# Layer 0's feed-forward up half: seven products on halved operands, its output through DRAM, and other buffer sizes

## The chip, the cores and the metric

The kernel runs on one core of a Trainium2 chip. The metric is device microseconds of one execution. Engines: TensorE (PE) for matmuls, VectorE (DVE), ScalarE (ACT), GpSimd (POOL), and SyncE (SP), whose queue issues most DMAs. Each engine works through its own queue in order and waits there on semaphores of the others.

## The reference

Two layers over 512 latent tokens (x) and 256 context tokens (ctx) of width 1024. Layer 0 mixes tokens by retention, layer 1 by differential attention; behind each mixer stands a gated feed-forward. Every sublayer is wrapped in RMS norms, with shift, scale and gate from SiLU(c) for the latents and SiLU(c_ctx) for the context:

```
u    = modulate(rms_norm(h, norm_g[l, 2]), shift, scale)
gate, val = split(u @ w_up)                  # 1024 -> 2 x 2816
h    = h + g * rms_norm((silu(dwconv3(gate) + b) * val) @ w_down, norm_g[l, 3])
```

dwconv3 is a convolution of three taps along the tokens, per channel. shift, scale and the gates of both layers are products of a 1024-vector with 6 x 1024 columns (adaLN). All is float32.

## The kernel before, in words

**Float32 on PE.** Every operand is split into a high half (a copy on ACT, rounded) and a low half (a subtraction on DVE, sometimes POOL): `split`, lines 58 to 60. A product is then three matmuls into the same PSUM bank: high x high, high x low, low x high (`mm3`, lines 96 to 99). A group with line 60 of the profile is thus a low half on DVE, one with line 59 a high half on ACT.

**Weights.** `W` (line 67) loads 128x1024 of raw weights by a DMA on SP into `wraw`, a pool of three buffers (line 63), and splits it into `wH`, `wL` (two buffers each) or, if `late`, into other tiles (`wlH`, `wlL`). With AHEAD a split stands earlier in the queues than the code has it.

**adaLN in the background.** 80 units are left over after the start; `ada_next(n)` (line 530) emits the next n. A unit loads 128x1024 of raw weights into the same `wraw` pool, and DVE multiplies and sums it against the conditioning vectors `cb` in one instruction (line 164) for each of one or two vectors: the output of the first goes to `adaj`, that of the last over `wraw` itself. The buffer is free after the last. In layer 0's retention (four heads, loop at 560 to 706) `ada_next(2)` stands behind the q and behind the k projection, `ada_next(3)` behind v, `ada_next(2)` behind the gates: 36 units. The other 44 lie in the up half, one pass of `between` behind each of its weights.

**Retention, per head.** q and then k: two column blocks c of 128 features, each eight contraction steps x three matmuls of 512 latent columns (into `psqx`) and of 256 context columns (`psqc`). Rotary operations on DVE (`ra`, `rb`, lines 591 to 593) need both column blocks. Then come gates, scores, values, and the normalised output, which goes to DRAM (`yTd`).

**Retention output and what follows** (`sublayer_out`, line 718). Latent tokens first, 16 contraction blocks; then, in a loop over the same 16 blocks, the context tokens, while a table `side` lets the other engines finish the latent tokens: gate and residual (`ft`, `hn`), norm (`xn`), PE transposes (`pst`) and modulation (`uf`) into the operand `UT`, whose halves lie in 24 tiles of 128x512 from the pool `s2`. The context tokens' norm and transposes come last (`ctx_part`), behind the first products of the next stage.

**Layer 0's up half** (`FFNUp`, line 282; called at 808 to 823). For each of 22 blocks f of 128 features, the gate unit and the value unit are each the sum over eight contraction blocks of matmuls with 512 and with 256 columns, into a bank each. Behind them: the convolution (ACT, and two operations on DVE, reading PSUM), SiLU on ACT, and the product with val on DVE, into tiles that stay in SBUF (`hTx`, `hTc`) for the down half (`sublayer_out` again, 22 contraction blocks).

A scheduler sets the order in each queue from the order in the code and the priorities; pools with few buffers add waits.

Of the kernel before, what the change touches and what calls it, by code (L numbers as in the profile page):

```python
# [30 lines left out]
def tile_hybrid_backbone(ctx: ExitStack, tc: tile.TileContext, A, out, dbg=None):  # L31
# [163 lines left out]
    class UT:  # L195
        def __init__(self):
            self.xH = [s2(F32R, name="uxH") for _ in range(KT)]
            self.xL = [s2(F32R, name="uxL") for _ in range(KT)]
            self.cH = self.cL = None

        def add_ctx(self):
            self.cH = [s2(F32R, (P, 2, 256), name="ucH") for _ in range(4)]
            self.cL = [s2(F32R, (P, 2, 256), name="ucL") for _ in range(4)]

        def part(self, p, k):

            if p == "c":
                return self.cH[k // 2][:, k % 2, :], self.cL[k // 2][:, k % 2, :]
            if isinstance(p, int) and p >= 4:
                o = slice((p - 4) * P, (p - 3) * P)  # L210
                return self.cH[k // 2][:, k % 2, o], self.cL[k // 2][:, k % 2, o]
            o = slice(p * P, (p + 1) * P) if isinstance(p, int) else {
                "x": slice(0, 512), "g0": slice(0, 256), "g1": slice(256, 512)}[p]
            return self.xH[k][:, o], self.xL[k][:, o]
# [8 lines left out]
    def to_u(ps, n, k, u, p, layer, sub_i, v):  # L223

        sh, sc = (0, 1) if sub_i == 0 else (3, 4)
        H, L = u.part(p, k)
        uf = t2((P, n), name="uf")
# [3 lines left out]
        else:  # L231
            nc.vector.tensor_scalar(out=uf, in0=ps, scalar1=a, scalar2=b, op0=ALU.mult, op1=ALU.add)
        split(H, L, uf)
# [127 lines left out]

    l0 = tc.tile_pool(name="l0", bufs=1)
# [32 lines left out]
    def ada_w(k):  # L395
        for kh in range(2):
            wada[k, kh] = W(A["ada0"][k * 2 + kh], late=k % 2 == 1, eng=nc.gpsimd if 2 * k + kh in (5, 9, 13, 4, 6, 0) else None, big=True)
# [69 lines left out]
    def first_ctx():  # L467
        U.add_ctx()
        norm_pair(psp, U, "c", xs[4:6], 0, 0)
# [8 lines left out]
    cb = l0p.tile([P, 2, 1024], F32, name="cb")  # L478
# [90 lines left out]
    for h in range(4):  # L569
# [3 lines left out]
        for qi in range(2):  # L573
# [29 lines left out]
            ada_next(2)  # L603
# [72 lines left out]
        ada_next(3)  # L676
# [25 lines left out]
        ada_next(2)  # L702
# [6 lines left out]
    def load_y(lo, hi):  # L709
        def at(k):  # L710
            y = s2(name="yin")
            nc.sync.dma_start(out=y[:, : hi - lo], in_=yTd[k, :, lo:hi])
# [5 lines left out]
    def sublayer_out(nk, unit, lx, lc, chunk, prev, dst_x, dst_c, layer, sub_i, hook, pre):  # L718
# [703 lines left out]
```

## Time and profile before

| | |
|---|---|
| median of three runs | 2206.97 us (2206.02 to 2208.29) |
| profiled execution | 2208.85 us, span 2207.0 us |
| PE busy | 2150.1 us, 97% |
| DVE, ACT, POOL busy | 56%, 38%, 11% |
| mean granted clock of PE | 0.986 |
| layer 0's up half | from 880.7 to about 1250 us |

The profile is one execution. A group row gives the mean length of one instruction; in a timeline, consecutive instructions of an engine overlap a little, so the distance of their starts is the cost of one. The word in brackets at the end of a timeline row is the idle time in front of it and what ended that. "issue to landing" of a DMA is from its issue on the queue until its data can be read.

### The profile page before, as it was taken

How to read it: one execution, taken by the hardware profiler on the slowest of the kernel's cores; microseconds unless marked ns; L12 is line 12 of the kernel's file. 1: busy time of each engine (PE TensorE's matmuls, PEld its weight loads, DVE VectorE, ACT ScalarE, POOL GpSimd, SP SyncE). 2: the span in 40 equal slices, each digit the busy share in tenths (PEclk: the TensorE clock that was granted, in tenths of full speed). 3: DMA queues.
4: the chain of work that ended last, by engine and by line, in shares of the span. 5: the costliest groups of instructions: out<-in, count | busy, mean ns of one | idle time of the engine just before them, and what ended most of it. 6: DMA issues, size and time to landing. Idle time of an engine off the chain costs nothing. (4 is left out here: it accounts for less than half of the span.)

```text
span 2207.0 us, 28221 instructions
## 1 busy us (share of the span) xinstructions
PE 2150.1 (97%) x11136; PEld 1834.2 (83%) x11136; DVE 1227.3 (56%) x1928; ACT 849.1 (38%) x1494; POOL 243.1 (11%) x310
## 2 busy tenths in 40 slices
PE   7999999999999999999999999999999789999998
PEld 6888888888888888888888888888888678888887
DVE  6656553553553348665445625767797686444524
ACT  5432233332332346322222324654455465333412
POOL 3001101100200101000000001021232151000000
PEclk8999999999999999999999999999999899999999
DMA  7232322322223366434444435611111332333333
GB/s 261 87 111 86 129 78 69 118 92 69 101 86 110 113 212 205 141 117 140 125 128 126 151 105 194 207 51 46 44 44 32 112 122 101 102 97 99 109 97 124
DMA packets 82732, 250.68 MB, mean 114 GB/s; under 512 B 10104, under 2 KB 13480, under 8 KB 82472
## 3 DMA queue, kind: packets, MB, share of 16 engines
q1 hardware_dynamic: 79880, 241.00, 34.0%
q0 software_dynamic: 2720, 7.89, 0.9%
q8 instruction: 87, 1.43, 0.3%
q14 instruction: 45, 0.37, 0.1%
HBM read 232.05 MB, written 16.80 MB: 113 GB/s over the span
## 5 line engine op out<-in xcount | busy, mean ns | idle before, releaser
L60 DVE TENSOR_TENSOR wL<-wraw,wH 128x1024 fp32r<-128x1024 f32 x233 | 286.1, 1228 | 504.9 <-ACT wH L59 503.3
L59 ACT ACTIVATE wH<-wraw 128x1024 fp32r<-128x1024 f32 x259 | 273.9, 1058 | 642.9 <-PE psa L99 182.9
L97 PE MATMUL psf<-uxH,wH 128*128 128x512 f32 (+1 forms) x672 | 258.7, 385 | 0.0
L98 PE MATMUL psf<-uxL,wH 128*128 128x512 f32 (+1 forms) x672 | 258.5, 385 | 0.0
L99 PE MATMUL psf<-uxH,wL 128*128 128x512 f32 (+1 forms) x672 | 258.1, 384 | 0.1
L97 PE MATMUL pso<-wH,lxH 128*128 128x512 f32 x432 | 168.3, 390 | 0.6 <-ACT grow L183 0.3
L98 PE MATMUL pso<-wL,lxH 128*128 128x512 f32 x432 | 168.1, 389 | 0.0
L99 PE MATMUL pso<-wH,lxL 128*128 128x512 f32 x432 | 168.1, 389 | 0.0
L164 DVE CUSTOM_DVE_ANT_0 wraw<-wraw,cb 128x1024 f32<-128x1024 f32 x80 | 97.6, 1223 | 96.9 <-DMA wraw<-in_ada_rest_dram 96.3
L99 PEld LDWEIGHTS psf<-uxH,wL 128*128 128x128 f32 x672 | 126.3, 188 | 25.6 <-DVE wL L60 0.3
L97 PEld LDWEIGHTS psf<-uxH,wH 128*128 128x128 f32 x672 | 126.5, 188 | 23.9
L98 PEld LDWEIGHTS psf<-uxL,wH 128*128 128x128 f32 x672 | 126.5, 188 | 23.4
L97 PE MATMUL psa<-wH,uxH 128*128 128x512 f32 x352 | 137.0, 389 | 0.0
L98 PE MATMUL psa<-wL,uxH 128*128 128x512 f32 x352 | 137.0, 389 | 0.0
L99 PE MATMUL psa<-wH,uxL 128*128 128x512 f32 x352 | 136.9, 389 | 0.0
L137 POOL TENSOR_SCALAR st<-st 128x1 f32<-128x1 f32 x42 | 27.7, 658 | 675.4 <-ACT junk L136 673.9
L97 PEld LDWEIGHTS pso<-wH,lxH 128*128 128x128 f32 x432 | 81.1, 188 | 17.8 <-ACT grow L183 0.6
L99 PEld LDWEIGHTS pso<-wH,lxL 128*128 128x128 f32 x432 | 81.1, 188 | 17.0
L99 PE MATMUL psf<-ucH,wL 128*128 128x256 f32 x336 | 95.1, 283 | 0.0
L98 PE MATMUL psf<-ucL,wH 128*128 128x256 f32 x336 | 95.1, 283 | 0.0
L98 PEld LDWEIGHTS pso<-wL,lxH 128*128 128x128 f32 x432 | 81.1, 188 | 16.6
L97 PE MATMUL psf<-ucH,wH 128*128 128x256 f32 x336 | 94.9, 282 | 0.0
(360 smaller groups left out, 5104.9 us busy)
## 6 DMA issues: line engine op xcount, KB each, us to landing
wraw<-in_up_dram SPq DMA_DIRECT2D x88, 512.0 KB, 3.6
wraw<-in_ada_rest_dram SPq DMA_DIRECT2D x80, 512.0 KB, 3.7
wraw<-in_down_dram SPq DMA_DIRECT2D x66, 512.0 KB, 3.6
wraw<-in_ret_in_dram SPq DMA_DIRECT2D x64, 512.0 KB, 3.7
wraw<-in_ret_out_dram SPq DMA_DIRECT2D x32, 512.0 KB, 3.8
wraw<-in_diff_in_dram SPq DMA_DIRECT2D x24, 512.0 KB, 3.6
wraw<-in_ada_dram SPq DMA_DIRECT2D x16, 512.0 KB, 7.3
wraw<-in_diff_out_dram SPq DMA_DIRECT2D x16, 512.0 KB, 3.8
```

Of the source, the lines that this page charges most:

```text
L59: nc.scalar.activation(out=h, in_=x, func=AF.Copy)
L60: (eng or nc.vector).tensor_tensor(out=l, in0=x, in1=h.bitcast(F32), op=ALU.subtract)
L97: nc.tensor.matmul(ps, l[0], r[0], start=first, stop=False)
L98: nc.tensor.matmul(ps, l[0], r[1], start=False, stop=False)
L99: nc.tensor.matmul(ps, l[1], r[0], start=False, stop=last)
L137: nc.gpsimd.tensor_scalar(out=s[:, 2:3], in0=s[:, 0:1], scalar1=s[:, 1:2], scalar2=EPS, op0=ALU.add, op1=ALU.add)
L164: nc.vector.tensor_tensor_reduce(out=o, in0=raw, in1=cb[:, v, :], scale=1.0, scalar=0.0, op0=ALU.mult, op1=ALU.add, accum_out=adaF[:, laye ...
```

## The change

The up half of layer 0 is rewritten as a scheme with seven products (`Seven`, `seven_w`, `ffn0`). The contraction is halved (features 0 to 511 and 512 to 1023), the columns are halved into the gate and the value block, and the tokens into two sets of 384 (two of every four latent blocks and one of two context blocks). In each pass f there are seven products of 4 contraction blocks x 3 matmuls x 384 columns, in the order 1, 6, 5, 7, 2, 3, 4.

- Token sums: per latent block of `sublayer_out`'s loop (`x_part`, at steps 6, 8, 10, 12) and for the context (`ctx_part`) one subtraction on POOL, three on DVE, and seven splits.
- Weight sums: four on POOL (S1 to S4, 128x512), seven splits of 128x512 per pass. The value block's raw weights go into an `s6` tile.
- Result sums: two copies of PSUM on ACT, five adds from PSUM on DVE, two adds on POOL, all of 384 columns. The gate lies in SBUF then, and the convolution reads it there.
- The result `val` goes to DRAM (`hd`) by a DMA on POOL's queue in each pass, and the down half loads it back on SP as it loads `yTd`.
- `ada_next` in retention goes from 2, 2, 3, 2 to 3, 3, 4, 3 per head (52 units); in the up half one unit stands behind each of the first 16 passes, and the last 12 behind them all.
- Pools: `s2` 48 to 31 buffers, `s6` 8 to 16; `UT` in eight `s6` tiles; the attention accumulators and some late weights in `s6`; `cb` in a pool of its own; the pool `l0` ends ahead of the up half.

The core of the diff:

```diff
-        return sp.tile(list(shape), dt, tag="s2", name=name, bufs=48)
+        return sp.tile(list(shape), dt, tag="s2", name=name, bufs=31)
 
     def s6(dt=F32, shape=(P, 1536), name="s6"):
-        return sp.tile(list(shape), dt, tag="s6", name=name, bufs=8)
+        return sp.tile(list(shape), dt, tag="s6", name=name, bufs=16)
...
-            ada_next(2)
+            ada_next(3)
...
-        ada_next(3)
+        ada_next(4)
...
-        ada_next(2)
+        ada_next(3)
...
-                4: lambda: (keep(2), sc(2)), 5: lambda: (keep(3), sc(3), tr(0)), 8: lambda: tr(1)}
+                4: lambda: (keep(2), sc(2)), 5: lambda: (keep(3), sc(3))}
+        if seven:
+            side |= {6 + 2 * q: lambda q=q: u.x_part(q, xn) for q in range(4)}
+        else:
+            side[5] = lambda: (keep(3), sc(3), tr(0))
+            side[8] = lambda: tr(1)
...
+        def sums(self, lo1, hi1, lo2, hi2, shape, at):
+
+            T = [t2(shape, name="T") for _ in range(2)]
+            a, b, c, d = (x[:, i] for x in T for i in range(2))
+            nc.gpsimd.tensor_tensor(out=b, in0=hi2, in1=hi1, op=ALU.subtract)
+            sub(a, hi1, lo1)
+            sub(c, hi2, a)
+            sub(d, lo2, c)
+            for i, x in ((1, lo1), (2, lo2), (3, hi2), (5, a), (6, c), (7, b), (4, d)):
+                split(at(self.H[i]), at(self.L[i]), x)
...
+    def seven_w(f):
+
+        g, v = load_raw(A["up"][0, 2 * f]), load_raw(A["up"][0, 2 * f + 1], True)
+        ops = {}
+        with tc.high_priority(offset=AHEAD):
+            g1, g2, v1, v2 = g[:, :512], g[:, 512:], v[:, :512], v[:, 512:]
+            S1, S2, S3, S4 = (t2(name="S") for _ in range(4))
+            pool = nc.gpsimd.tensor_tensor
+            pool(out=S1, in0=v1, in1=v2, op=ALU.add)
+            pool(out=S2, in0=S1, in1=g1, op=ALU.subtract)
+            pool(out=S3, in0=g1, in1=v1, op=ALU.subtract)
+            pool(out=S4, in0=g2, in1=S2, op=ALU.subtract)
+            for i, x in zip(ORDER, (g1, S2, S1, S3, g2, S4, v2)):
+                if i in (1, 2):
+                    H, L = (wp.tile([P, 1024], F32R, tag=t, name=t, bufs=2)[:, :512] for t in ("wH", "wL"))
+                else:
+                    H, L = s2(F32R, name="opH"), s2(F32R, name="opL")
+                split(H, L, x)
+                ops[i] = H, L
+        return ops
...
+            def product(i, p):
+                if i not in banks:
+                    banks[i] = bank("psf")
+                o = {"x": slice(0, 256), "c": slice(256, 384), "all": slice(0, 384)}[p]
+                H, L = ops[i]
+                for k in range(4):
+                    s = slice(k * P, k * P + P)
+                    mm3(banks[i][:, o], (H[:, s], L[:, s]), u.at(i, k, p), k == 0 and p != "c", k == 3 and p != "x")
...
+            if f == 0:
+                for i in ORDER[:4]:
+                    product(i, "x")
+                ctx_part()
+                for i in ORDER[:4]:
+                    product(i, "c")
+            for i in ORDER:
+                if f > 0 or i in ORDER[4:]:
+                    product(i, "all")
+                ps = banks[i][:, :384]
+                add = lambda o, a, b, e=nc.vector: e.tensor_tensor(out=o, in0=a, in1=b, op=ALU.add)
+                if i == 1:
+                    p1 = tmp("p1")
+                    nc.scalar.activation(out=p1, in_=ps, func=AF.Copy)
+                elif i == 6:
+                    u2 = tmp("u2")
+                    add(u2, ps, p1)
+                elif i == 5:
+                    p5, u4 = tmp("p5"), tmp("u4")
+                    nc.scalar.activation(out=p5, in_=ps, func=AF.Copy)
+                    add(u4, u2, p5, nc.gpsimd)
+                    if f + 1 < NF:
+                        nxt.append(seven_w(f + 1))
+                elif i == 7:
+                    u3, v = tmp("u3"), wide("val")
+                    add(u3, ps, u2)
+                    add(v[:, :, 1, :], three(u3), three(p5), nc.gpsimd)
+                elif i == 2:
+                    g = wide("gate3")
+                    add(g[:, :, 0, :], three(ps), three(p1))
+                elif i == 3:
+                    add(g[:, :, 1, :], three(ps), three(u4))
+                else:
+                    add(v[:, :, 0, :], three(ps), three(u3))
+            flat = lambda x: x.rearrange("p a b c -> p (a b c)")
+            g, v = flat(g), flat(v)
+            c = flat(wide("conv3"))
+            w0, w1, w2, cbias = (cw[:, 0, f, i : i + 1] for i in range(4))
+            nc.scalar.activation(out=c, in_=g, func=AF.Identity, scale=w1, bias=cbias)
+            for a, b in ((0, 512), (512, 768)):
+                nc.vector.scalar_tensor_tensor(out=c[:, a + 1 : b], in0=g[:, a : b - 1], scalar=w0, in1=c[:, a + 1 : b],
+                                               op0=ALU.mult, op1=ALU.add)
+                nc.vector.scalar_tensor_tensor(out=c[:, a : b - 1], in0=g[:, a + 1 : b], scalar=w2, in1=c[:, a : b - 1],
+                                               op0=ALU.mult, op1=ALU.add)
+            nc.scalar.activation(out=c, in_=c, func=AF.Silu)
+            nc.vector.tensor_tensor(out=v, in0=v, in1=c, op=ALU.mult)
+            nc.gpsimd.dma_start(out=hd[f], in_=v)
+            ada_next(1 if f < NF - 6 else 0)
+            ops = nxt[0] if nxt else None
...
+    ffn0(u, first, ctx_part)
     ada_next(len(ada_list))
...
-        NF, lambda k: A["down"][0, k], lhs_x(lambda k: F.hx[k]), lhs_c(lambda k: F.hc[k]), 5, lambda t: rows(h1d, t),
+        NF, lambda k: A["down"][0, k], lhs_x(load_y(hd, 0, 512)), lhs_c(load_y(hd, 512, 768)), 5, lambda t: rows(h1d, t),
```

**SP's queue in retention**, a head's v projection to the next head's k projection. `in_ret_in` is a retention weight, `in_ada_rest` an ada unit. Before:

```order
L64 DMA wraw<-in_ada_rest_dram 128x1024 x3
L64 DMA wraw<-in_ret_in_dram 128x1024 x4
L64 DMA wraw<-in_ada_rest_dram 128x1024 x2
L64 DMA wraw<-in_ret_in_dram 128x1024 x2
L64 DMA wraw<-in_ada_rest_dram 128x1024 x2
L64 DMA wraw<-in_ret_in_dram 128x1024 x3
L64 DMA wraw<-in_ada_rest_dram 128x1024 x2
```

After:

```order
L64 DMA wraw<-in_ada_rest_dram 128x1024 x4
L64 DMA wraw<-in_ret_in_dram 128x1024 x4
L64 DMA wraw<-in_ada_rest_dram 128x1024 x3
L64 DMA wraw<-in_ret_in_dram 128x1024 x2
L64 DMA wraw<-in_ada_rest_dram 128x1024 x3
L64 DMA wraw<-in_ret_in_dram 128x1024 x3
L64 DMA wraw<-in_ada_rest_dram 128x1024 x3
```

Each group of ada loads is longer by one, and the groups behind the q projection, the k projection and the gates are now as long as the pool is wide.

**DVE's queue behind the q projection of a head** (from the second `ra`, in front of which stands the first `rb`). Rows with `adaj` or `wraw` at line 164 are reductions of ada units. Before:

```order
L591 TENSOR_TENSOR ra<-psqx,rcos 128x512
L593 TENSOR_TENSOR ra<-ra,rb 128x512
L592 TENSOR_TENSOR rb<-psqx,rsin 128x512
L164 ISA adaj,adaF<-wraw,cb 128x1024
L164 ISA adaF 128x1
L164 ISA adaj,adaF<-wraw,cb 128x1024
L164 ISA adaF 128x1
L593 TENSOR_TENSOR ra<-ra,rb 128x512
L60 TENSOR_TENSOR qxL<-ra,qxH 128x512
L60 TENSOR_TENSOR wL<-wraw,wH 128x1024
L164 ISA wraw,adaF<-wraw,cb 128x1024
L164 ISA adaF 128x1
```

After:

```order
L593 TENSOR_TENSOR ra<-psqx,rcos 128x512
L595 TENSOR_TENSOR ra<-ra,rb 128x512
L594 TENSOR_TENSOR rb<-psqx,rsin 128x512
L164 ISA adaj,adaF<-wraw,cb 128x1024
L164 ISA adaF 128x1
L164 ISA adaj,adaF<-wraw,cb 128x1024
L164 ISA adaF 128x1
L595 TENSOR_TENSOR ra<-ra,rb 128x512
L60 TENSOR_TENSOR qxL<-ra,qxH 128x512
L164 ISA adaj,adaF<-wraw,cb 128x1024
L164 ISA adaF 128x1
L164 ISA wraw,adaF<-wraw,cb 128x1024
```

A third unit's first reduction stands ahead of the first unit's second one, and the weight's low half (`wL`) that stood in between is no longer there.

**DVE's queue in the up half**, one pass. Before (`hT` is the product with val):

```order
L328 TENSOR_TENSOR hTx<-psf,conv 128x512
L164 ISA wraw,adaF<-wraw,cb 128x1024
L164 ISA adaF 128x1
L328 TENSOR_TENSOR hTc<-psf,conv 128x256
L60 TENSOR_TENSOR wL<-wraw,wH 128x1024
L323 SCALAR_TENSOR_TENSOR conv<-psf,cw,conv 128x511
L325 SCALAR_TENSOR_TENSOR conv<-psf,cw,conv 128x511
L164 ISA adaj,adaF<-wraw,cb 128x1024
L164 ISA adaF 128x1
L164 ISA wraw,adaF<-wraw,cb 128x1024
L164 ISA adaF 128x1
L60 TENSOR_TENSOR wL<-wraw,wH 128x1024
```

After (`opL`, `wL` are low halves of operands, `u`, `gate`, `val` the result sums):

```order
L935 TENSOR_TENSOR u_9852<-psf,p_9837 128x384
L60 TENSOR_TENSOR opL<-S,opH 128x512 x4
L935 TENSOR_TENSOR gate_9941<-psf,p_9837 128x3x128
L60 TENSOR_TENSOR opL<-wraw,opH 128x512
L935 TENSOR_TENSOR u_9924<-psf,u_9852 128x384
L60 TENSOR_TENSOR wL<-wraw,wH 128x512
L935 TENSOR_TENSOR gate_9941<-psf,u_9868 128x3x128
L965 SCALAR_TENSOR_TENSOR conv_9971<-gate_9941,cw,conv_9971 128x511
L935 TENSOR_TENSOR val<-psf,u_9924 128x3x128
L965 SCALAR_TENSOR_TENSOR conv_9971<-gate_9941,cw,conv_9971 128x255
L967 SCALAR_TENSOR_TENSOR conv_9971<-gate_9941,cw,conv_9971 128x511
L967 SCALAR_TENSOR_TENSOR conv_9971<-gate_9941,cw,conv_9971 128x255
```

One pass now has seven low halves of 128x512 in place of two of 128x1024, five adds, and convolution operations that read SBUF.

**POOL's queue in the up half**, from one pass's first add to the next pass's; before, it held only 12 small operations in that whole stretch. After (`S` are weight sums):

```order
L935 TENSOR_TENSOR u_10339<-u_10323,p_10338 128x384
L892 TENSOR_TENSOR S<-wraw 128x512
L893 TENSOR_TENSOR S<-wraw,S 128x512
L935 TENSOR_TENSOR val<-u_10395,p_10338 128x3x128
L890 TENSOR_TENSOR S<-wraw 128x512
L891 TENSOR_TENSOR S<-S,wraw 128x512
L971 DMA hd<-val 128x768
```

Four sums of 512 columns, two adds of 384 and one DMA issue stand there per pass.

## Rows read from the trace of the kernel before

**Rows 1.** The page: busy time by engine, and PE's slices (tenths busy).

```profile
PE 2150.1 (97%) x11136; PEld 1834.2 (83%) x11136; DVE 1227.3 (56%) x1928; ACT 849.1 (38%) x1494; POOL 243.1 (11%) x310
...
PE   7999999999999999999999999999999789999998
```

**Rows 2.** Busy time by stretch, the up half: us, busy (instructions) by engine, clock, DMA.

```profile
880.70:1250.00 369.30, 369.30 (x2134) 326.98 (x2132) 207.32 (x332) 108.27 (x171) 7.19 (x12) 1.00 0.42 134
```

**Rows 3.** Timeline of PE at 229 us: start, length, engine, line, op, out<-in.

```profile
229.28 0.39 PE L99 MATMUL psqx<-uxH,wL 128*128 128x512 f32 x1
229.51 0.28 PE L97 MATMUL psqc<-ucH,wH 128*128 128x256 f32 x1
229.62 0.28 PE L98 MATMUL psqc<-ucL,wH 128*128 128x256 f32 x1
```

**Rows 4.** Timeline of DVE between head 1's q and k projections.

```profile
240.75 0.69 DVE L592 TENSOR_TENSOR rb<-psqx,rsin 128x512 f32<-128x512 f32 x1 [0.53 <-PE psqx L99]
241.36 0.68 DVE L591 TENSOR_TENSOR ra<-psqx,rcos 128x512 f32<-128x512 f32 x1
...
243.15 1.22 DVE L164 CUSTOM_DVE_ANT_0 adaj<-wraw,cb 128x1024 bf16<-128x1024 f32 x1
...
244.29 1.22 DVE L164 CUSTOM_DVE_ANT_0 adaj<-wraw,cb 128x1024 bf16<-128x1024 f32 x1
...
245.44 0.69 DVE L593 TENSOR_TENSOR ra<-ra,rb 128x512 f32<-128x512 f32 x1
246.04 0.69 DVE L60 TENSOR_TENSOR qxL<-ra,qxH 128x512 fp32r<-128x512 f32 x1
...
247.78 1.22 DVE L164 CUSTOM_DVE_ANT_0 wraw<-wraw,cb 128x1024 f32<-128x1024 f32 x1
```

**Rows 5.** Groups of DVE by shape: busy us, mean ns, idle before.

```profile
L325 DVE SCALAR_TENSOR_TENSOR conv<-psf,cw,conv 128x511 f32<-128x511 f32 x44 | 33.0, 750 | 1.3
...
L325 DVE SCALAR_TENSOR_TENSOR conv<-psf,cw,conv 128x255 f32<-128x255 f32 x22 | 10.6, 483 | 0.8
...
L60 DVE TENSOR_TENSOR PL<-ptmp,PH 128x384 fp32r<-128x384 f32 x8 | 4.4, 555 | 0.0
```

**Rows 6.** Timeline of POOL and DVE at 1525 us, and of DVE at 1567 us.

```profile
1525.30 1.29 POOL L856 TENSOR_TENSOR ds<-ds,dsin 128x512 f32<-128x512 f32 x1
...
1525.44 1.97 DVE L1147 SCALAR_TENSOR_TENSOR E<-E,nm 128x768 f32<-128x768 f32 x1
...
1566.95 1.02 DVE L1147 SCALAR_TENSOR_TENSOR E<-E,nm 128x768 f32<-128x768 f32 x1
```

**Rows 7.** Timeline of DVE, then of PE, behind the retention output stage.

```profile
880.48 1.88 DVE L271 TENSOR_TENSOR ft<-pso,G 128x512 f32<-128x512 f32 x3
...
888.33 0.88 DVE L220 TENSOR_SCALAR xn<-hn,st 128x512 f32<-128x512 f32 x2 [1.03 <-POOL st L138]
...
891.68 1.91 PE L242 MATMUL pst<-ident,xn 128*128 128x128 f32 x16
```

**Rows 8.** Busy time by stretch, end of the context loop (columns as in group 2).

```profile
830.00:880.00 50.00, 49.12 (x232) 40.57 (x231) 39.08 (x70) 34.29 (x76) 7.75 (x12) 1.00 0.64 213
```

**Rows 9.** Timeline of PE: last psqx matmul of q, first psqc, first psqx of k.

```profile
240.26 0.39 PE L99 MATMUL psqx<-uxH,wL 128*128 128x512 f32 x1
240.49 0.28 PE L97 MATMUL psqc<-ucH,wH 128*128 128x256 f32 x1
...
243.36 0.40 PE L97 MATMUL psqx<-uxH,wH 128*128 128x512 f32 x1
```

**Rows 10.** The page: the high half on ACT, and the raw weight's DMA.

```profile
L59 ACT ACTIVATE wH<-wraw 128x1024 fp32r<-128x1024 f32 x259 | 273.9, 1058 | 642.9 <-PE psa L99 182.9
...
wraw<-in_ret_in_dram SPq DMA_DIRECT2D x64, 512.0 KB, 3.7
```

**Rows 11.** Busy time by stretch: an idle of PE in layer 1, and behind it.

```profile
1821.60:1824.30 2.70, 0.00 (x1) 0.01 (x1) 2.70 (x5) 1.84 (x5) 0.00 (x0) 1.00 1.08 339
...
1827.00:1832.00 5.00, 5.00 (x25) 5.00 (x25) 4.20 (x8) 3.75 (x9) 2.21 (x1) 0.50 0.07 26
```

More of the change, by code (lines that the diff above doesn't have):

```diff
@@ L232, in to_u @@
             nc.vector.tensor_scalar(out=uf, in0=ps, scalar1=a, scalar2=b, op0=ALU.mult, op1=ALU.add)
+    def to_u(ps, n, k, u, p, layer, sub_i, v):
+        H, L = u.part(p, k)
+        uf = t2((P, n), name="uf")
+        modulated(uf, ps, k, layer, sub_i, v)
         split(H, L, uf)
@@ L357, in lhs_c @@
         return at
+    cbs = tc.tile_pool(name="cbs", bufs=1)
+    cb = cbs.__enter__().tile([P, 2, 1024], F32, name="cb")
     l0 = tc.tile_pool(name="l0", bufs=1)
@@ L716, in tile_hybrid_backbone, with sublayer_out @@
     rows = lambda a, t: a[t * P : (t + 1) * P, :]
-    def sublayer_out(nk, unit, lx, lc, chunk, prev, dst_x, dst_c, layer, sub_i, hook, pre):
+    def sublayer_out(nk, unit, lx, lc, chunk, prev, dst_x, dst_c, layer, sub_i, hook, pre, seven=False):
         G = load_gate(0, chunk, 0)
@@ L745, in ahead @@
                 if j == len(wcs) and j <= k + 2:
-                    wcs.append(W(unit(j), "s6" if j % 2 == 0 else False))
+                    wcs.append(W(unit(j), j % 3 == 2 if seven else "s6" if j % 2 == 0 else False))
         ahead(0)
@@ new lines, in ffn0, with three @@
+    def ffn0(u, ops, ctx_part):
+        pool = tc.tile_pool(name="ff", bufs=1)
+        fp = pool.__enter__()
+        wide = lambda name: fp.tile([P, 3, 2, P], F32, tag=name, name=name)
+        for f in range(NF):
+            banks = {}
+            nxt = []
+            def product(i, p):
+                if i not in banks:
+                    banks[i] = bank("psf")
+                o = {"x": slice(0, 256), "c": slice(256, 384), "all": slice(0, 384)}[p]
+                H, L = ops[i]
+                for k in range(4):
+                    s = slice(k * P, k * P + P)
+                    mm3(banks[i][:, o], (H[:, s], L[:, s]), u.at(i, k, p), k == 0 and p != "c", k == 3 and p != "x")
+            def three(x):
+                return x[:, :384].rearrange("p (a c) -> p a c", a=3)
+            tmp = lambda name: s2(shape=(P, 384), name=name)
+            if f == 0:
[4 more added lines that the diff above has]
+                    product(i, "c")
+            for i in ORDER:
+                if f > 0 or i in ORDER[4:]:
[23 more added lines that the diff above has]
+                    add(g[:, :, 1, :], three(ps), three(u4))
+                else:
+                    add(v[:, :, 0, :], three(ps), three(u3))
[14 more added lines that the diff above has]
+            ops = nxt[0] if nxt else None
+        pool.__exit__(None, None, None)
@@ L809, in tile_hybrid_backbone @@
[L809 to L823 removed]
+    l0.__exit__(None, None, None)
+    ffn0(u, first, ctx_part)
     ada_next(len(ada_list))
@@ L1320, in tile_hybrid_backbone @@
     hp = {t: load_h(rows(h3d, t)) for t in range(4)}
-    keep = [(k, W(A["down"][1, k], True), lx(k)) for k in range(NF - late, NF)]
+    keep = [(k, W(A["down"][1, k], "s6"), lx(k)) for k in range(NF - late, NF)]
     for t in (2, 0, 1, 3):
```

124 lines of the change are left out of this document (75 added, 49 removed).

## The prediction

> **What bounds the kernel now.** I read the page's busy table and its slices first [rows 1]: TensorE (PE) is busy 97% of the span and its slices read 9 almost throughout; the gaps lie in the first slice and late in layer 1. So matmul work taken off PE counts in full, and every wait put in front of PE counts in full too. I then read the stage that is rewritten [rows 2]: in the 369.3 us of the up half PE never stops, DVE is busy 207 us and POOL 7 us. Last I looked for places where PE's cover over its next weight is thin, since the edit also moves adaLN work (the "ada units") into retention.
>
> **Part 1, fewer matmuls in the up half: minus 45 us, on the path.** A 512-column matmul starts 0.227 us after the one before, a 256-column one 0.120 us [rows 3]. Before: 22 feature blocks x 2 x 8 x 3 = 1056 of each, 366.7 us, which is the window of [rows 2] but for some transposes. After: 384 columns lie midway between, 0.1736 us (an estimate). Block 0 does four products in two pieces: 48 matmuls of 256 columns (5.8 us) and 48 of 128 (about 0.067 each if the line goes on, 3.2 us). The other 150 products have 12 matmuls each: 1800 x 0.1736 = 312.5 us. Together 321.5 us, 45 less. From the second block on, PE needs 84 x 0.1736 = 14.6 us per block.
>
> **Part 2, the operand and result sums: plus 24 us.** The sums that save a product land on DVE and POOL. Consecutive DVE operations of 512 columns step 0.60 us [rows 4], about 0.085 under their listed duration, so I take that off the others. Per block DVE has seven subtractions (the low halves) of 512: 4.2 us; five adds from PSUM of 384 (0.555 less 0.085 [rows 5]): 2.35; four scalar-tensor-tensor operations (0.75 and 0.48 [rows 5]): 2.1; one 768-wide product, about 0.93 (1.02 [rows 6]); one ada reduction in the first 16 blocks, 1.15 [rows 4]. Together 10.7 us, under PE's 14.6. But DVE and POOL are not independent. In [rows 6] DVE's 768-wide operation, with both inputs in SBUF, takes 1.02 us with POOL quiet and 1.97 us when it starts 0.14 us behind a POOL tensor-tensor of 512; POOL thus held it back until 1.09 us after its own start. POOL now does four sums of 512 and two of 384 in each block, 4 x 1.09 + 2 x 0.82 = 6.0 us of such holding. The DVE operations with two SBUF inputs are the low halves, the convolution (its gate now lies in SBUF and no longer in PSUM), the product and the ada reduction: 8.4 us. One after the other that is 14.4 us, PE's own period, before the 2.35 us of PSUM reads find a place. If none of these lie beside POOL, the period is 16.8 us (15.6 without ada); if all do, PE's 14.6. I take 16.0 and 14.8, since the PSUM adds sit between the others in DVE's queue and POOL's two adds wait for DVE's results: 16 x 1.4 + 6 x 0.2 = 24 us. Ends: 0 and 16 x 2.2 + 6 x 1.0 = 41.
>
> The Trainium skill states this as a rule (page "SBUF — State Buffer", section "Who interferes with whom"): a DVE instruction with two SBUF inputs contends with a GpSimd instruction that reads SBUF, and the pair of ports is an exclusive lock. It speaks against this change, and the trace agrees (1.97 against 1.02 us). Without it the up half would run at PE's pace, which is the third case below.
>
> **Part 3, entry to the up half: plus 11 us.** Before, 48 matmuls of 512 columns (10.8 us) stood between the last down-projection matmul and the context transposes, and no wait appeared [rows 7]. After, only 48 of 256 (5.8 us) stand there, to 886.5 on the old clock, while the last normalised context tile is ready at 889.2 [rows 7] and now queues behind up to four low halves of the first operands on DVE. So PE idles 2.7 to 4.5 us, transposes 1.9 us, then waits for four scalings, three sums and splits: nine DVE operations of 0.60 stand up to the one that the second context product needs, 5.4 us and 0.5 for the scaling, less 0.8 of work that it has. That makes 8 to 10 us, 14 with POOL's lock; I take 11. The extra token sums inside the context loop (DVE is busy 39.1 of 50 us there [rows 8] and gets about 13 more) and the startup: 3 (0 to 6). The down half reads its input back from DRAM; those loads are issued tiles ahead, as the retention output's are now, and I cost them at nothing (up to 5 if they queue behind the 12 last ada loads).
>
> **Part 4, the ada units moved into retention: plus 60 us, and 12 for the clock.** The raw weight pool has three buffers, and each ada unit takes one until its last DVE reduction has read it. Two units at a time left one buffer to the next weight; three leave none. In SP's queue the next weight therefore waits for the first unit's second reduction, and in DVE's queue this stands behind the rotary operations of the projection that PE has only just finished. The cover is the context matmuls of that projection: from 240.5 to 243.36, 2.9 us [rows 9]. Against it, by DVE's rows at that place [rows 4]: rb, ra, ra, rb (240.75 to 243.15, four steps), two adaj (to 245.44), ra and qxL (1.2), a third adaj (1.15), the reduction (1.22), so the buffer is free at 249.0; then 3.7 us from issue to landing and 1.06 us for ACT's high half [rows 10], at 253.8. PE could have begun at 243.36: 10.4 us, and 0.8 more since the third matmul needs DVE's low half. Heads 1 to 3 pay 11.2 each: 33.6. In these heads the weight behind the second group of three has 11 us of cover against the same chain of 13.2: 2.2 each, 6.6. Head 0 lacks the gate weights between: both its places have the short cover, with fewer rotary operations in front (9.7 and 10.1). Sum 60. Bounds: 45 if the scheduler's chain overlaps better than row by row, 70 if DVE runs late. PE's granted clock after an idle of 2.7 us in layer 1 was 0.50, its lower level, 1.2 GHz, for some us [rows 11]; five long idles at 2.4 us each (a stretch of 5 us at half rate loses 2.5): 12, from 0 to 17.
>
> **Sum.** -45 + 24 + 11 + 3 + 60 + 12 = +65 on the profiled run's 2208.85 us; the median of the three runs shown is 1.9 us lower: 2272. Layer 1 keeps its order but for where the attention accumulators lie: 0 (10 either way).
>
> **The rivals.** *Faster:* the weight after the ada units is not held. It decides at the cover: if the loads find a buffer 10 us earlier than I read (a wait on the buffer that ends with the first reduction of a unit, or reductions that DVE reaches before the rotary operations), retention costs nothing, as with two units now, where no wait shows [rows 1]. Then 2207 - 45 + 11 + 3 + 0 to 24 = 2176 to 2200. Against it: the order is fixed in the queues and DVE's rows have the durations. Chance 0.13, a third of it near or inside no change. *Up half at PE's pace:* the DVE operations that read PSUM fill the time that POOL holds, retention waits as forecast: 2272 - 24 = 2248. For it: DVE's plain sum is 4 us under PE's. Chance 0.22. *Lock fully serial:* period 16.8, and POOL's DMA issues are pushed back too: 2272 + 17 + 3 = 2292. For it: with ada the exclusive part alone fills PE's period. Chance 0.15. My forecast between these: 0.50. *The change doesn't do what it says* (a 384-column matmul as dear as one of 512): 1800 x 0.053 = 95 more; [rows 3] speak against it, left out.
>
> **How the numbers follow.** The range takes the second and third cases and the bounds of retention and clock: 2222 to 2306; the faster case and a little above are left out. About 0.2% (4.4 us) is what a measurement can tell from no change. Faster 0.10 and same 0.04 come from the first rival and a corner of the second with short waits; slower 0.86.
>
> **What would show it.** In retention: PE idle of about 11 us in front of a psqx matmul in each of heads 1 to 3, released by ACT's high half of a weight or its DMA, with the granted clock at 0.50 behind it; the raw weight's issue on SP right behind an ada reduction on DVE. In the up half: about 16 us per block, DVE's low halves at 1.2 us and over where POOL adds run, and PE waiting for opL, wL or a bank that the adds free. At the entry: two idles around the 16 transposes. I am wrong if retention has no PE idle (then the time is under 2207), or if blocks take over 17 us.

## The result, and the profile after

The changed kernel takes 2327.32 us (median of four, 2323.86 to 2329.51) against 2206.49 us of the kernel before on the same chip: 1.0547 times, with a 95% interval of 1.0529 to 1.0565. The forecast was 2272 us, 2222 to 2306: the sign is right, the growth (121 us) is almost twice the 65 that were forecast, and the time lies above the range.

The page of the profiled execution (2327.78 us, span 2326.1), rows as in [rows 1]:

```profile
PE 2153.5 (93%) x10920; PEld 1852.1 (80%) x10920; DVE 1437.2 (62%) x2140; ACT 901.2 (39%) x1602; POOL 448.4 (19%) x468
...
PE   7889899899979999798889889999999888999998
```

PE has 216 matmuls fewer and yet is busy as long as before, since parts of them run at the lower clock, and its slices show holes from the second one on. POOL is busy almost twice as long. Where the time went, from the starts and ends of the stages in PE's timeline (first and last matmul into the stage's PSUM tiles; us):

| stage | before | after | difference | forecast |
|---|---|---|---|---|
| start, to the first `psqx` matmul | 74.3 | 77.6 | +3.3 | 0 to 1 |
| retention, to the last `psy` transpose | 674.0 | 744.1 | +70.1 | +72 |
| retention output, to the first `psf` | 132.4 | 134.4 | +2.0 | +2 to 3 |
| up half, to the last `psf` | 368.7 | 400.9 | +32.2 | -10 |
| to the down half's first `pso` | 0.1 | 7.4 | +7.3 | 0 |
| down half, to the first `psq` | 183.9 | 187.2 | +3.3 | 0 |
| layer 1 | 767.0 | 768.1 | +1.1 | 0 |

The stages are those of one profiled execution each. The start varies by some 3 us between profiles of kernels that have the same program there (74.1 to 77.6), layer 1 by 6 (765.1 to 771.1), so a difference of that size in one stage means little. Who PE waited for, in us, times, longest (the table of waits, PE):

```profile
PE psqx L97 <- ACT wH L59: 39.4, 4, 10.4
PE psf L99 <- DVE wL L60: 28.3, 24, 4.2
PE psf L99 <- DVE opL L60: 10.5, 12, 2.6
PE psa L97 <- ACT wH L59: 10.1, 4, 8.5
PE pso L97 <- ACT lxH L59: 7.0, 1, 7.0
```

The first and fourth row are retention, the second and third the up half, the fifth the entry to the down half.

**Retention.** DVE's timeline behind the q projection of head 1, the place of [rows 4], then the rows of SP, ACT and PE that answer:

```profile
269.00 0.69 DVE L594 TENSOR_TENSOR rb<-psqx,rsin 128x512 f32<-128x512 f32 x1 [3.06 <-PE psqx L99]
...
274.90 1.22 DVE L164 CUSTOM_DVE_ANT_0 adaj<-wraw,cb 128x1024 bf16<-128x1024 f32 x1
...
276.04 1.22 DVE L164 CUSTOM_DVE_ANT_0 wraw<-wraw,cb 128x1024 f32<-128x1024 f32 x1
...
277.30 3.82 SPq L64 DMA_DIRECT2D wraw<-in_ret_in_dram  x3
...
281.04 1.06 ACT L59 ACTIVATE wH<-wraw 128x1024 fp32r<-128x1024 f32 x1 [5.51 <-DMA wraw<-in_ret_in_dram]
...
282.14 0.80 PE L97 MATMUL psqx<-u,wH 128*128 128x512 f32 x1 [10.37 <-ACT wH L59]
```

The chain is the forecast one, link by link: the first unit's second reduction ends at 277.26, SP issues the weight at 277.30, ACT splits it at 281.04, and PE starts after 10.37 us of idle (10.4 were forecast). Behind it PE runs at its lower clock for a while (granted clock 0.58 in the mean of the first stretch, 1.00 in the second; columns as in [rows 11]):

```profile
282.30:286.00 3.70, 3.66 (x9) 2.45 (x10) 2.27 (x2) 1.06 (x1) 0.00 (x0) 0.58 0.62 216
287.00:289.00 2.00, 2.00 (x11) 1.65 (x10) 0.00 (x0) 0.00 (x0) 0.00 (x0) 1.00 0.49 197
```

**The up half.** The stretch of [rows 2], then the entry, then one steady pass:

```profile
956.10:1357.00 400.90, 353.23 (x1913) 336.24 (x1912) 365.91 (x451) 147.06 (x266) 200.02 (x159) 0.96 0.34 115
...
954.00:984.00 30.00, 17.21 (x90) 15.22 (x88) 25.51 (x38) 17.36 (x39) 13.26 (x15) 0.73 0.26 90
...
1059.60:1077.10 17.50, 15.38 (x84) 14.43 (x84) 16.34 (x20) 6.28 (x11) 8.97 (x7) 1.00 0.32 114
```

DVE is now busy 366 of 401 us, and in this pass 16.3 of 17.5; PE works off its 84 matmuls and waits. Pass by pass (starts of PE's matmuls, 84 apart), the second to the fourth pass still take 14.6 us and the fifth 15.4; then come eleven with an ada unit, at 17.1 to 18.3 and mostly 17.7, four without one, at 16.4, and the last two, in which DVE also has reductions of the last ada units, at 21.0 and 16.9. The groups of DVE in 1000 to 1240 us show which of its work became long (columns as in [rows 5]):

```profile
L60 DVE TENSOR_TENSOR opL<-S,opH 128x512 fp32r<-128x512 f32 x54 | 79.2, 1524 | 0.0
L967 DVE SCALAR_TENSOR_TENSOR conv<-gate,cw,conv 128x511 f32<-128x511 f32 x14 | 23.8, 1702 | 0.0
...
L965 DVE SCALAR_TENSOR_TENSOR conv<-gate,cw,conv 128x511 f32<-128x511 f32 x14 | 10.8, 772 | 15.1 <-ACT conv L963 15.1
L935 DVE TENSOR_TENSOR val<-psf,u 128x384 f32<-128x384 f32 x14 | 7.7, 550 | 0.0
```

The low halves of the weight sums take 1.52 us each instead of 0.68; the convolution's second operation 1.70 instead of 0.75. The adds that read PSUM keep their 0.55. The third row has something the forecast left out: 15.1 us in 14 passes in which DVE waits for ACT's convolution step.

### The profile page after: what moved, and what is told of

It is laid out like the page before. It is cut to its first block, busy times and chain, and to the rows that moved or that the text cites. A ratio compares the mean times of both kernels' runs of the same rounds, so it can differ in the third digit from the quotient of the medians.

```text
span 2326.1 us, 28562 instructions
## 1 busy us (share of the span) xinstructions
PE 2153.5 (93%) x10920; PEld 1852.1 (80%) x10920; DVE 1437.2 (62%) x2140; ACT 901.2 (39%) x1602; POOL 448.4 (19%) x468
## 5 line engine op out<-in xcount | busy, mean ns | idle before, releaser
L60 DVE TENSOR_TENSOR wL<-wraw,wH 128x1024 fp32r<-128x1024 f32 (+1 forms) x238 | 271.4, 1141 | 438.4 <-ACT wH L59 436.4
L59 ACT ACTIVATE wH<-wraw 128x1024 fp32r<-128x1024 f32 (+1 forms) x264 | 259.6, 985 | 580.3 <-PE psa L99 177.8
L97 PE MATMUL psa<-wH,u 128*128 128x512 f32 x528 | 207.3, 393 | 10.1 <-ACT wH L59 10.1
L98 PE MATMUL psa<-wL,u 128*128 128x512 f32 x528 | 207.2, 392 | 4.2 <-DVE wL L60 4.2
L99 PE MATMUL psa<-wH,u 128*128 128x512 f32 x528 | 206.7, 391 | 0.0
L99 PE MATMUL psf<-tH,opL 128*128 128x384 f32 (+2 forms) x452 | 154.4, 342 | 11.0 <-DVE opL L60 10.5
L98 PE MATMUL psf<-tL,opH 128*128 128x384 f32 (+2 forms) x452 | 152.9, 338 | 1.4 <-DVE tL L60 1.4
L97 PE MATMUL psf<-tH,opH 128*128 128x384 f32 (+2 forms) x452 | 152.9, 338 | 0.0
L99 PE MATMUL psf<-u,wL 128*128 128x512 f32 (+1 forms) x336 | 127.4, 379 | 0.2 <-DVE wL L60 0.2
L97 PE MATMUL psf<-u,wH 128*128 128x512 f32 (+1 forms) x336 | 127.3, 379 | 0.0
L98 PE MATMUL psf<-u,wH 128*128 128x512 f32 (+1 forms) x336 | 127.3, 379 | 0.0
L97 PEld LDWEIGHTS psa<-wH,u 128*128 128x128 f32 x528 | 100.0, 189 | 32.2 <-ACT wH L59 11.5
L99 PEld LDWEIGHTS psa<-wH,u 128*128 128x128 f32 x528 | 99.8, 189 | 20.7
```

The costliest lines, as they stand in the source:

```text
L59: nc.scalar.activation(out=h, in_=x, func=AF.Copy)
L60: (eng or nc.vector).tensor_tensor(out=l, in0=x, in1=h.bitcast(F32), op=ALU.subtract)
L97: nc.tensor.matmul(ps, l[0], r[0], start=first, stop=False)
L98: nc.tensor.matmul(ps, l[0], r[1], start=False, stop=False)
L99: nc.tensor.matmul(ps, l[1], r[0], start=False, stop=last)
```

## The experiments

Times in brackets after a label are the kernel's, then that of the kernel before on the same chip. Where no interval stands it is one execution; four of the changed kernel lie between 2323.86 and 2329.51. "Less than the changed kernel" is against its median, 2327.32, which was measured apart from these runs.

**Retention alone: e1_ret_ada (2280.37; 2209.92).** The kernel before with

```diff
-            ada_next(2)
+            ada_next(3)
...
-        ada_next(3)
+        ada_next(4)
...
-        ada_next(2)
+        ada_next(3)
```

> The kernel before, with only the ada units moved: 3, 3, 4, 3 per head of retention instead of 2, 2, 3, 2; the up half stays as it was and takes the 28 units that are left. My theory (a weight waits for the buffer of an ada unit): the four heads get longer by about 70 us as in the changed kernel, so 2265 to 2285 us, with PE idle of about 10 us ahead of the k projection of each head. Rival (the waits in retention come from the smaller s2 pool or another part): 2207 us, give or take 4.

Measured: 70.5 us more. Retention takes 744.5 us, as in the changed kernel (744.1), with the same wait ahead of head 1's k projection:

```profile
277.50 0.79 PE L97 MATMUL psqx<-uxH,wH 128*128 128x512 f32 x1 [10.46 <-ACT wH L59]
```

The ada units are the cause by themselves, not the smaller `s2` pool.

**One raw buffer more: e2_wraw4 (2265.72; 2209.92).** The changed kernel with

```diff
-        return sp.tile(list(shape), dt, tag="s2", name=name, bufs=31)
+        return sp.tile(list(shape), dt, tag="s2", name=name, bufs=29)
...
-... tag="wraw", name="wraw", bufs=3)
+... tag="wraw", name="wraw", bufs=4)
```

> The changed kernel with one raw weight buffer more (4 instead of 3) and two s2 tiles fewer to make room. My theory: the fourth load no longer waits for an ada unit, the waits in retention go and the up half stays at about 401 us: 2327 less 65 to 70, so 2255 to 2265 us. Rival (DVE is late in retention whatever the buffers, since the third unit is in its queue): at least half of the 70 us stays, 2290 us or more.

Measured: 61.6 us less than the changed kernel, retention 682.8 us. The waits ahead of the k projections are gone: in retention PE is idle for 5.8 of 682.8 us, and for 54.7 of 744.1 in the changed kernel (first row the changed kernel, second e2):

```profile
77.60:821.70 744.10, 689.35 (x3230) 574.36 (x3230) 369.65 (x624) 216.98 (x376) 64.66 (x138) 0.96 0.30 97
...
74.90:757.70 682.80, 677.00 (x3230) 569.22 (x3229) 367.59 (x625) 216.32 (x377) 71.89 (x139) 1.00 0.33 107
```

The 9 us that are left over the 674.0 of before lie in head 0 (156 against 150 us) and behind head 3. So it is the buffer that held the weight, and not DVE's longer queue.

**All sums on DVE: e3_sums_dve (2266.31; 2209.92).** The changed kernel with

```diff
-            pool = nc.gpsimd.tensor_tensor
+            pool = nc.vector.tensor_tensor
...
-                    add(u4, u2, p5, nc.gpsimd)
+                    add(u4, u2, p5)
...
-                    add(v[:, :, 1, :], three(u3), three(p5), nc.gpsimd)
+                    add(v[:, :, 1, :], three(u3), three(p5))
```

> The changed kernel with the four weight sums and the two result adds of each pass on DVE instead of POOL; nothing else. Lock theory (each POOL operation that reads SBUF stops DVE's two-input operations for its whole length): DVE's plain work rises from 10.7 to 14.1 us per pass, the 6 us of holding go, the period falls from 17.7 to about 15.2 with an ada unit and 14.6 without: 16 x 2.5 + 6 x 1.8 = 51 us less, about 2276. Load theory (DVE is simply overloaded, POOL's part costs it nothing): 3.3 us more per pass, 22 x 3.3 = 73 us more, about 2400.

Measured: 61.0 us less, 53.9 of them in the up half (347.0 us). DVE has six operations more in each pass, and the pass is shorter. In the steady part PE no longer waits at all (stretch 1080 to 1180), and a low half takes what it takes alone:

```profile
1080.00:1180.00 100.00, 100.00 (x579) 100.00 (x578) 96.58 (x173) 43.92 (x75) 3.79 (x7) 1.00 0.44 138
...
L60 DVE TENSOR_TENSOR opL<-S,opH 128x512 fp32r<-128x512 f32 x68 | 44.4, 683 | 0.0
```

The load theory falls. What is left of the up half over PE's own 321.5 us, 25.5 us, is the entry: every pass behind the first takes PE's 14.6 us. These are e3's entry and a stretch behind it:

```profile
953.00:980.00 27.00, 15.10 (x82) 12.66 (x81) 23.59 (x41) 16.54 (x38) 5.74 (x9) 0.75 0.28 100
...
980.00:1080.00 100.00, 100.00 (x562) 100.00 (x563) 94.76 (x169) 42.62 (x73) 2.80 (x5) 0.95 0.42 135
```

PE is idle for 11.9 us. Behind that it has no wait, but works at the lower clock for a while (granted clock 0.50 from 980 to 990 us, 0.95 in the mean of the second row).

**One more POOL read: e5_pool_read (2307.67; 2209.92).** The changed kernel with, behind the fourth weight sum,

```diff
+            if fpx:
+                pool(out=fpx[0], in0=g1[:, :480], in1=g2[:, :480], op=ALU.add)
```

> The changed kernel with one more POOL add of 128x480 per pass, both inputs from SBUF, into a tile that nobody reads, behind the fourth weight sum. Lock theory: each holds DVE for about 1.0 us, 21 passes, +17 to +23 us, about 2347. Load theory: POOL has time (8 of 17.7 us busy) and nobody waits for the result: 2327, give or take 5.

Measured: 20 us *less* than the changed kernel, 14.0 of them in the up half (386.9 us); the rest is spread over stages whose program is the same, the start alone 2.4. Both theories miss, mine with the wrong sign. The rows tell why the sum of holds is no good measure. First a pass of the changed kernel, DVE and POOL at the low halves of the weight sums:

```profile
1062.55 3.19 DVE L60 TENSOR_TENSOR opL<-S,opH 128x512 fp32r<-128x512 f32 x1
...
1062.91 1.03 POOL L935 TENSOR_TENSOR u<-u,p 128x384 f32<-128x384 f32 x1
1063.88 1.30 POOL L892 TENSOR_TENSOR S<-wraw 128x512 f32<-128x512 f32 x1
1065.88 1.60 POOL L893 TENSOR_TENSOR S<-wraw,S 128x512 f32<-128x512 f32 x1 [0.70 <-DVE opL L60]
...
1066.27 1.78 DVE L60 TENSOR_TENSOR opL<-S,opH 128x512 fp32r<-128x512 f32 x1
```

One low half is held through two POOL operations in a row, another through the third. Now the run with the extra add (`junkp`); DVE's rows begin with the last of the four low halves:

```profile
1078.38 1.50 DVE L60 TENSOR_TENSOR opL<-S,opH 128x512 fp32r<-128x512 f32 x1
1079.80 0.55 DVE L939 TENSOR_TENSOR gate<-psf,p 128x384 f32<-128x384 f32 x1
1080.27 1.31 DVE L60 TENSOR_TENSOR opL<-wraw,opH 128x512 fp32r<-128x512 f32 x1
1081.49 0.55 DVE L939 TENSOR_TENSOR u<-psf,u 128x384 f32<-128x384 f32 x1
1081.96 1.31 DVE L60 TENSOR_TENSOR wL<-wraw,wH 128x512 fp32r<-128x512 f32 x1
...
1076.52 1.39 POOL L896 TENSOR_TENSOR junkp<-wraw 128x480 f32<-128x480 f32 x1
1077.87 1.46 POOL L939 TENSOR_TENSOR u<-u,p 128x384 f32<-128x384 f32 x1
1079.29 1.73 POOL L893 TENSOR_TENSOR S<-wraw 128x512 f32<-128x512 f32 x1
1080.98 1.74 POOL L894 TENSOR_TENSOR S<-wraw,S 128x512 f32<-128x512 f32 x1
```

The extra add and the result add `u` take the place beside the low halves, the weight sums start later, DVE and POOL take turns, and each of these two sums has a PSUM read of DVE beside it for about a third of its time (0.55 of 1.73 us). In the changed kernel they start too early for that: POOL's queue is held by the result's DMA until DVE has done the product with `val` (57.2 us of waits in 13 passes between 1000 and 1250 us), and just then DVE goes into four low halves in a row.

**Pushes that read nothing: e6_pool_write (2327.01; 2208.71), e9_pool_push (2324.00; 2210.64), e13_push2 (2316.55; 2207.69).** Memsets on POOL instead of the add; the last two set the convolution's tile, which ACT overwrites before anybody reads it:

```diff
+                    c = flat(wide("conv3"))
+                    nc.gpsimd.memset(c, 0.0)
```

(e13 has the memset twice; in e6 it stood where e5 has its add.)

> The changed kernel with one POOL memset of 128x480 per pass, which reads nothing, where the run before had an add that reads SBUF and made the kernel 20 us faster. Alignment theory (what POOL costs DVE hangs on where POOL's operations fall; the extra operation only pushed the adds and sums behind it beside DVE's PSUM reads and its idle time): a shorter push without a hold of its own, a gain of 3 to 20 us, 2307 to 2324. If the read itself brought the gain: 2327, give or take 4. If the push by half a microsecond is too short to matter: 2327 as well.

> The changed kernel with one POOL memset of 128x768 per pass (about 0.8 us, reads nothing) right behind the DMA issue of the result, where the extra add stood in the run that came out 20 us faster; it sets a tile that ACT overwrites before anybody reads it. Alignment theory (the extra add only moved POOL's result add and two weight sums to a later place, beside DVE's PSUM reads): most of the 20 us again, 2304 to 2315. If the reading of the extra add brought the gain: 2327, give or take 4.

> The changed kernel with two POOL memsets of 128x768 per pass, one ahead of the first result add and one behind it, about 1.5 us in all, reading nothing. Alignment theory (the first two weight sums must start behind DVE's four low halves in a row to fall beside its PSUM reads): 0.8 us of push was too short, 1.5 us is as long as the extra add that gained 20 us, so 2300 to 2314. If the read itself brought that gain: 2327, give or take 4.

e6 tells nothing: the scheduler put its 21 memsets, which depend on nothing, all into retention (723 to 735 us), so it is a repeat of the changed kernel, to 0.3 us. e9's 3 us less are within the spread of the changed kernel; its up half takes 398.3 us, where the changed kernel has 400.9 and e6 399.9, so no gain is clear. e13 takes 11 us less, 6 of them in the up half (394.8 us, against 386.9 of the extra add). Both are longer than the alignment theory had them (2304 to 2315 and 2300 to 2314). A push of 1.5 us brings at most half of what the add brought: in e13 the two sums follow each other without a gap and hold the last of the four low halves through both (it takes 3.25 us), so they were not pushed behind all four, while behind the add POOL and DVE alternate. So where POOL's operations fall seems to matter, and so does who gets the turn; both were seen in rows, and neither was isolated.

**Half of the sums each: e10_s_pool (2309.83; 2210.64) and e11_adds_pool (2280.88; 2210.64).** Only the two result adds to DVE, and only the four weight sums to DVE (the first or the other two lines of the diff of e3).

> The changed kernel with only the two result adds moved to DVE; the four weight sums stay on POOL. If every POOL read of SBUF costs DVE its hold and nothing lies beside: DVE 10.7 + 0.9, 4.4 of hold, 1.2 of waiting for ACT, period 17.2 with an ada unit, 16.0 without, 11 us less: 2316. Alignment theory: the sums are no longer tied to the adds in POOL's queue and part of them falls beside PSUM reads: 2280 to 2305.

> The changed kernel with only the four weight sums moved to DVE; the two result adds stay on POOL. DVE 10.7 + 2.4, 1.6 of hold: 14.7 per pass, just PE's pace if DVE's wait for ACT is hidden, 2266 to 2275; with that wait of 1.2 us in every pass as now: 15.9, 2285 to 2292.

Measured: 17 and 46 us less than the changed kernel; both lie between the two values that were expected. The table has for each variant how slow the low halves of the weight sums are, and what all of DVE's operations with two inputs in SBUF last over their mean lengths in e3, added up from 43 us behind the start of the up half to its end:

| | up half, us | mean of `opL<-S`, ns | over e3's lengths, us | matmuls, 1080 to 1180 us |
|---|---|---|---|---|
| changed kernel | 400.9 | 1524 | 101 | 479 |
| e9, e13: pushes | 398.3, 394.8 | 1452, 1322 | 97, 94 | 489, 492 |
| e10: weight sums on POOL | 387.6 | 1150 | 76 | 510 |
| e5: one more read | 386.9 | 1009 | 87 | 526 |
| e11: result adds on POOL | 353.8 | 738 | 17 | 569 |
| e3: nothing on POOL | 347.0 | 683 | 0 | 579 |

The order is nearly the same in all columns, but it is no line. From the changed kernel to e5 DVE loses 14 us less and the up half is 14.0 us shorter, though POOL reads once more per pass; for e9 and e13 it is 4 and 7 against 3 and 6. e10 loses 25 us less, but DVE has two adds more in each pass (0.94 us). In e11 and e3 DVE is no longer what PE waits for in most passes.

**Both cures, and further: e4_both, e7_entry, e8_tail, e12_spread.** e4 is e2 and e3 together. e7 adds to it `ORDER[:6]` for `ORDER[:4]` in the first pass; e8 adds to e7 one `ada_next(1)` per contraction block of the down half in place of all ahead of it. e12 is e4 with

```diff
-            ada_next(3)
+            ada_next(3 if h else 2)
...
-            ada_next(1 if f < NF - 6 else 0)
+            ada_next(2 if f % 3 == 2 else 1)
```

> The changed kernel with four raw weight buffers (two s2 tiles fewer) and all sums on DVE: the two runs that gave 2265.7 and 2266.3 together. If the two causes are independent: 2327 - 61.6 - 61.0 = 2204, range 2198 to 2212, the same as the kernel before within 0.3%. If one hides part of the other (DVE short of time in retention or the entry): 2215 or more.

> As the run with both, and six instead of four of the first pass's products run on the latent tokens ahead of the context tokens' part, 2.9 us more work of PE in front of their transposes. If the entry's waits are lack of cover, as in my third part: 2 to 4 us less, and less of the half clock, so 3 to 7 us below the run with both. If DVE's queue there (sums and splits of the context) sets the end: no change.

> As the run with six products first, and the last ada units are emitted one per contraction block in the down half instead of all ahead of it, so that its first weight and its first input on SP no longer wait behind 12 loads. If those loads are what PE waits for at the down half (4.6 to 7 us): 4 to 7 us below the run before it. If the wait is the way of the last result through DRAM: no change.

> The run with four raw weight buffers and all sums on DVE, with the ada units spread anew: two instead of three behind q and k of head 0, one behind every pass of the up half and two behind every third, so that four instead of twelve (counting two of the last pass) are left in front of the down half. From that run's trace: head 0 5 us longer than before, the down half 8 us longer. If both come from the ada units and DVE has the time in the up half: 2204 less 8 to 13, 2191 to 2197. If the second units slow the passes: 2202 or more.

| | us | before | ratio (95%) |
|---|---|---|---|
| e4_both | 2204.40 | 2208.71 | 0.9986 (0.9976 to 0.9995) |
| e7_entry | 2208.18 | 2208.71 | 0.9995 (0.9983 to 1.0007) |
| e8_tail | 2205.84 | 2208.71 | 0.9989 (0.9979 to 0.9998) |
| e12_spread | 2201.67 | 2210.64 | 0.9959 (0.9945 to 0.9974) |

The two causes add up: 2204 was worked out and 2204.40 measured. The changed kernel and all runs made from it also set `dynamic_dma_scratch_size=2048`, a line of the diff that its core does not show; e4 has it too and is as fast as the kernel before.

e7 was to gain 3 to 7 us and gains nothing (its up half takes 347.1 us against 345.2). PE's idle at the entry does fall, from 11.2 to 8.8 us, but the last wait ends as late as before (24.74 us behind the start of the up half in e4, 24.95 in e7), and it is for DVE's low half `tL` in both: DVE's queue sets that end. What was gained went to the clock, which was at its lower level (granted clock under 0.75) for 20.5 us at e4's entry and 27.0 at e7's. That length varies between profiles of the same entry (24.0 in e12, which has e4's, and 23.5 in e8, which has e7's), so the loss is not shown to be e7's own.

e8 takes 2.3 us less than e7, where 4 to 7 were expected. Its down half is 4 us shorter (187.8 against 191.9), but its layer 1 is 5.6 longer, most of which is within what layer 1 varies by. e12 is 0.4% faster than the kernel before, the best of all: retention is back at 675.0 us and the up half at 346.3, 22 less than before. It misses its forecast of 2191 to 2197, for its down half still takes 194.6 us against 183.9. In its first 14 us PE waits for a low half (1.4) and for the up half's last result sum, which reads PSUM (3.9), and runs partly at the lower clock; spreading the ada units did not mend that, and what does stays open.

## Why the prediction was right and wrong

**Part 1, right.** A 384-column matmul starts 0.173 us after the one before (0.1736 forecast), and in e3 the 84 of a pass take 14.56 us.

**Part 4, right in mechanism and size.** Forecast 60 for the waits and 12 for the clock; measured 70.1 in the changed kernel and 70.5 alone. The waits ahead of the k projections of heads 1 to 3 were 10.3 to 10.4 against 10.4, and the chain has the forecast links. By parts it is less close: PE's idle in retention grew by 54 us (54.7 against 0.6), not 60, and 16 us, not 12, are left for the lower clock; that the two misses cancel is luck. This part was worked out from the order of two queues and DVE's rows.

**Part 2, the step that failed: how much of POOL's holding would lie beside DVE's PSUM reads.** The holding itself was right: [rows 6] were read rightly, and taking POOL's reads away brings 53.9 us. The Trainium skill's rule (page "SBUF — State Buffer", section "Who interferes with whom") is that a DVE instruction with two SBUF inputs contends with a GpSimd instruction that reads SBUF. The traces agree: 1.52 us for the low halves of the weight sums, 0.68 with nothing on POOL. The size was not right: 24 forecast, 54 measured. I took 16.0 us per pass with an ada unit and 14.8 without, between the ends, on the argument that the PSUM adds sit between the others in DVE's queue. Most passes take 17.7 and 16.4, above my upper ends of 16.8 and 15.6, and blocks over 17 us were my own sign of being wrong.

Two things were missing. First, what POOL's queue waits for decides what it lies beside: the DMA of the result waits for DVE's product, so that u4 and the two sums behind it come out exactly at DVE's four low halves in a row, and none beside a PSUM read. In the pass shown only the second result add lies beside one (1069.65 to 1071.04 us). The order of both queues stood in the part on the change, so this could have been seen. Second, DVE waits about 1.1 us in each pass for ACT's convolution step, since the next operation in its queue needs it; I had summed DVE's work as if it never waited. 10.7 of work, 5.7 of holds and 1.1 of waiting are 17.5. (The 5.7 are what DVE's operations last over their lengths in e3, per pass between 1060 and 1190 us.) So the 6.0 us of holding in the forecast came almost in full, and nothing much of them was hidden.

**Part 3, right in kind and too short.** 11 forecast, 25.5 measured by e3, where the entry is all that is left. In the stretch of the changed kernel shown above, PE worked 17.2 of 30 us at a mean clock of 0.73: I had counted the waits (about 12 us in e3) and forgotten to charge the half clock that I had charged in retention. And the down half's input, costed at nothing with up to 5 if the 12 ada loads were in front, cost 7.3: the case in the brackets was the one that came, and dearer.

```profile
1320.04 33.34 SPq L64 DMA_DIRECT2D wraw<-in_ada_rest_dram  x11
...
1354.47 1.21 DVE L164 CUSTOM_DVE_ANT_0 wraw<-wraw,cb 128x1024 f32<-128x1024 f32 x1
...
1355.72 0.33 SPq L64 DMA_DIRECT2D wraw<-in_down_dram  x1
1356.16 0.37 SPq L714 DMA_DIRECT2D yin<-hd  x1
...
1364.36 0.79 PE L97 MATMUL pso<-wH,lxH 128*128 128x512 f32 x1 [7.04 <-ACT lxH L59]
```

The first weight of the down half stands behind the ada loads on SP. It is issued as an ada unit's reduction ends on DVE (1355.68), as in retention, and PE starts 8.6 us after its issue. Behind this idle PE runs at the lower clock (granted clock 0.50 from 1364.4 to 1369.4 us). Five us at half rate lose 2.5 of the 3.3 us that the down half itself is longer (an estimate); it has no wait of its own of more than 0.2 us.

**The sum.** Of the 55 us between the forecast and the measured time, 30 are Part 2's, 14 Part 3's and 7 the way into the down half. The small rest is spread over the start and the down half.

**The rivals.** "Lock fully serial" (chance 0.15) was the right one for the up half, and was still priced too low, since its period of 16.8 us had no wait in it. "Up half at PE's pace" held for the second to the fourth pass alone. The faster rival fell with e1: the weight is held, in the order read from the queues.

## What to carry to other kernels

Count the buffers of a pool against the longest run of loads that nobody needs soon: as soon as the run is as long as the pool, the next urgent load waits for the last reader of that run's first load, and one buffer more (e2) or one load fewer (the kernel before) cures it. Work moved to an idle engine is not free if its operations hold those of a busy one, as POOL's sums held DVE's here; before pricing it midway, look in both queues at what releases it and what the other engine does at that moment. A budget per pass needs the waits between the engines in it, not only the work. And where PE idles for some us, price the lower clock behind the idle as well as the idle: at the entry it cost about as much.

## What the runs showed of the hardware

A DVE subtraction with both inputs in SBUF, 0.68 us alone, took 3.19 us while two POOL operations ran one right behind the other beside it, though its recorded start is 0.36 us ahead of the first. In e9 one took 4.25 us, beside three in a row: it is the last of the four low halves in the first row here (its recorded start is 1097.93), and a third POOL operation, the next weight sum, runs from 1100.32 to 1101.62.

```profile
1096.12 6.05 DVE L60 TENSOR_TENSOR opL<-S,opH 128x512 fp32r<-128x512 f32 x4
...
1098.10 1.04 POOL L936 TENSOR_TENSOR u<-u,p 128x384 f32<-128x384 f32 x1
1099.08 1.30 POOL L892 TENSOR_TENSOR S<-wraw 128x512 f32<-128x512 f32 x1
```

I had expected the one that starts first to be done first, and a hold of one operation at most. The Trainium skill (page "SBUF — State Buffer", section "Who interferes with whom") says for one of its cases that whoever issues first gets the pair. These rows don't look like that, but a recorded start need not be the first read. In e5 the two engines alternate instead; why is open.

A POOL memset, which reads nothing, held nobody: in e13 a low half keeps its 0.68 us beside it. The Trainium skill has it so too (the same page and section: a GpSimd instruction that only writes does not contend with a DVE instruction with two SBUF inputs).

```profile
1062.12 0.68 DVE L60 TENSOR_TENSOR opL<-S,opH 128x512 fp32r<-128x512 f32 x1
...
1062.45 0.76 POOL L946 MEMSET conv<- 128x768 f32 x1
```

One more POOL read per pass made the up half 14 us shorter in a kernel that is slow because of POOL reads (e5, one execution). What such an operation costs or gains here hangs on what DVE does beside it.
